# Queueing the uses of gathered rows behind points of the third and fourth groups, a set number for each point

## The chip, the cores and the metric

The kernel runs on one core of a Trainium2 chip. A core has TensorE for matrix products, VectorE and ScalarE for arithmetic by elements and by rows, GpSimd, which here issues the gathers, and SyncE, which issues most of the other transfers; 16 DMA engines carry all transfers. The metric is the device time of one execution in microseconds (us). Before the change it is 3744.16 us, the median of three runs from 3742.86 to 3752.52.

## The reference

One layer of a diffusion backbone over 1024 latent tokens and 256 context tokens, in float32, with 1024 channels. Only the latent stream is put out.

```python
z_lat = modulate(h_lat, sh_a, sc_a) @ w_in          # and z_ctx
att_lat = block_attention(q_l, concat([k_c, k_l]), concat([v_c, v_l]))   # 8 heads, 1280 keys
s5_lat, s5_ctx = s5_mixer(...)                      # state-space branch, two directions
merged = sigmoid(gate_mla) * att + sigmoid(gate_s5) * s5_out
h_lat = layer_norm(ALPHA * h_lat + g_a * (merged @ w_out))
f_lat = peer(modulate(h_lat, sh_f, sc_f), ...)
h_lat = layer_norm(ALPHA * h_lat + g_f * f_lat)
```

The part that matters here is `peer`. For each token 8 heads choose 16 of 16384 experts each, so 128 experts. Expert e has a row u[e] and a row v[e] of 1024 numbers. The output of a token is the sum over its experts of g * gelu(u[e] . x) * v[e].

## The kernel before

The 1024 tokens are eight blocks of 128, handled in four groups: `GROUPS = ((0,), (1, 2), (3, 4, 5), (6, 7))`. For each group `front` traces, in this order: `attention` (eight heads, and for each head and block one pass over 1280 keys: score matmuls, row maximum, exponential, transposes, product with the values), `gates` (four column slices, and in each the blocks of the group), `close` (output projection, two layer norms, and the next group's query projection in `prepare`), and then `route`, a generator that finds each token's 128 experts. The routing of a group is stepped inside the attention of the next: two steps after each head (`TSTEP`). Inside the gates of the third and fourth groups `spread` steps, which writes the gates of the routed experts into dense tables, mostly on ScalarE with small matmuls on TensorE.

The experts are applied in three ways. Blocks 2 to 5 (`DENSE`) multiply with all experts in `dense`, which runs last and takes about the last 40% of the time. Blocks 6 and 7 (`VEC`) are gathered beside it. Blocks 0 and 1 are gathered beside the groups, in `retrieve([0, 1])`, and this is what the change touches. In `score` (L1264 on) each of 128 steps gathers one row u for each of the block's 128 tokens (an indirect DMA on GpSimd's queue, 128 rows of 4 KB, L1269), and VectorE multiplies it with the tokens and sums (L1273): one use. In `weighted` each of 128 steps gathers rows v (L1349), and TensorE adds them, weighted, into two banks with four matmul calls (L1354): one use as well. All rows land in one pool of six buffers (`RB = 6`), so a gather waits until the use of the row six before it is done. The order in which `retrieve` traces the uses is: 128 scores of block 0, then 32 weighted rows of block 0, then two scores of block 1 to one weighted row of block 0, then the remaining weighted rows, those of block 1 last. The weighted rows of a block need all of its scores.

The order in each engine's queue is made when the program is built: a list scheduler goes through the traced instructions with an estimate of their times, and where an engine is free it takes the ready instruction of the best priority. `retrieve([0, 1])` is traced after the fourth group's `front`, which is traced under `tc.high_priority` (`PRIO`), so its uses come behind all work of the groups and fill what that leaves. On the chip each queue then runs in that order. `tc.issue_after(ins)` adds an edge to each instruction of its block that is on the engine of `ins`: it is placed in the queue behind `ins`, with no wait for its end.

Before the change such edges stand on scores alone, by `HOLDS`: block 0's first 36 scores are free and the others are behind `p2`, the end of the third group's query projection (`prepare(2)`, L774); block 1's first 100 are free and the others are behind `p3`, that of the fourth group. The entries that name steps of routing (`r1`, `r2`) begin at 164 and 228 and so hold nothing. The uses of block 6 are behind `t3`. The weighted rows on TensorE have no edge.

```python
HOLDS = {0: [(M0, S0)] + [("r1.%d" % h, S0 + P0 * (h + 1)) for h in range(8)],
         1: [(M1, S1)] + [("r2.%d" % h, S1 + P1 * (h + 1)) for h in range(8)],
         6: [("t3", 0)]}
```

Of the kernel before, what the change touches and what calls it, by code (L numbers as in the profile page):

```python
# [17 lines left out]
MUL, ADD, SUB = ALU.mult, ALU.add, ALU.subtract  # L18
# [57 lines left out]
P1 = 128  # L76
M0 = "p2"
M1 = "p3"
HOLDS = {0: [(M0, S0)] + [("r1.%d" % h, S0 + P0 * (h + 1)) for h in range(8)],
         1: [(M1, S1)] + [("r2.%d" % h, S1 + P1 * (h + 1)) for h in range(8)],  # L80
         6: [("t3", 0)]}
KENG = ((), (), (), ())
GENG = ((), (), (), ())
EVERY = (1, 2, 1)
# [4 lines left out]
def block_kernel(ctx: ExitStack, tc: tile.TileContext, a: dict, out: bass.AP):  # L89
# [91 lines left out]
            marks["last"] = V.scalar_tensor_tensor(x, x, rstd[:, j:j + 1], b, op0=MUL, op1=ADD)  # L181

    marks = {}

    def transpose8(x, put, tag="tp"):

        for h in range(2):
            pt = bank(tag, "tp", (128, 4, 128))
            for j in range(4):
                k = 4 * h + j  # L190
                PE.transpose(pt[:, j, :], x[:, k * 128:(k + 1) * 128], eye)
            put(h, pt)


# [40 lines left out]
    def product(o, x, w, n):  # L235

        for k in range(n):
            PE.matmul(o, x[0][:, k, :], w[0][:, k, :], start=(k == 0), stop=False)
            PE.matmul(o, x[1][:, k, :], w[0][:, k, :], start=False, stop=False)
            PE.matmul(o, x[0][:, k, :], w[1][:, k, :], start=False, stop=(k == n - 1))  # L240


    xt = []
# [544 lines left out]
    def attention(grp, att):  # L788
        nt = len(grp)
        ntok = 128 * nt  # L790
        Q, cqT, rq = R["q"]
        A = pool("A")
        late = []

        def finish(P, sm3, vt, i, h):

            rs = cols.tile([128, 1], F32, tag="smx", name="smx")
            V.tensor_reduce(rs, sm3, axis=AX.X, op=ADD)
            V.reciprocal(rs, rs)
            PT = A.tile([128, NT, 128], F32, tag="PT", name="PT")  # L800
            for b0, b1 in ((0, 4), (4, 8), (8, 10)):
                pt = bank("tp", "pt", (128, 4, 128))
                for j in range(b0, b1):
                    PE.transpose(pt[:, j - b0, :], P[:, j * 128:(j + 1) * 128], eye)
                S.copy(PT[:, b0:b1, :], pt[:, 0:b1 - b0, :])
            po = bank("mm", "po")
            for j in range(NT):
                PE.matmul(po[:, 0:128], PT[:, j, :], vt[:, j, :], start=(j == 0), stop=(j == NT - 1))  # L808
            S.activation(att[i][:, h * 128:(h + 1) * 128], po[:, 0:128], func=AF.Copy, scale=rs)

        for pr in range(4):
            qn = []
            qr = A.tile([128, ntok], F32, tag="qr", name="qr")
            rl = A.tile([128, ntok], F32R, tag="rl", name="rl")
            q2 = rl.bitcast(F32)
            wq = wload(a["w_uq"][pr], [128, 3, 512])
            for j in (2, 3, 0, 1):
                ps = bank("mm", "pq")
                for k in range(3):
                    PE.matmul(ps[:, 0:ntok], wq[:, k, j * 128:(j + 1) * 128], cqT[:, k, :], start=(k == 0), stop=(k == 2))  # L820
                if j < 2:
                    qh = A.tile([128, ntok], F32R, tag="qnh", bufs=2, name="qnh")
                    ql = A.tile([128, ntok], F32R, tag="qnl", bufs=2, name="qnl")
                    split(qh, ql, ps[:, 0:ntok])
                    qn.append((qh, ql))
                else:
                    V.tensor_tensor(qr if j == 2 else q2, ps[:, 0:ntok], rq[:, j - 2, :], op=MUL)
            V.tensor_tensor(qr, qr, q2, op=ADD)
            rh = A.tile([128, ntok], F32R, tag="rh", name="rh")
            split(rh, rl, qr)  # L830
            for hh in range(2):
                h = 2 * pr + hh
                lo = 64 * hh
                st = A.tile([128, ntok], F32R, tag="qst", bufs=2, name="qst")
                S.copy(st[0:64], rh[lo:lo + 64].bitcast(F32))
                V.tensor_copy(st[64:128], rl[lo:lo + 64].bitcast(F32))
                kt = wload(k_d[h], [128, KEYS])
                kc = []
                for c in range(3):
                    c0, w = 512 * c, (512 if c < 2 else 256)  # L840
                    kh = A.tile([128, w], F32R, tag="kh%d" % c, name="kh")
                    kl = A.tile([128, w], F32R, tag="kl%d" % c, name="kl")
                    split(kh, kl, kt[:, c0:c0 + w], GP if c in KENG[GROUPS.index(grp)] else V)
                    kc.append((kh, kl))
                vt = A.tile([128, NT, 128], F32, tag="vt", bufs=2, name="vh")
                SY.dma_start(vt, v_d[h])
                qh, ql = qn[hh]
                for i in range(nt):
                    ts = slice(i * 128, (i + 1) * 128)
                    mx = cols.tile([128, 3], F32, tag="mx", name="mx")  # L850
                    pS = []
                    for c in range(3):
                        c0, w = 512 * c, (512 if c < 2 else 256)
                        cs = slice(c0, c0 + w)
                        ps = bank("S", "pS")[:, 0:w]
                        kh, kl = kc[c]
                        PE.matmul(ps, qh[:, ts], kh, start=True, stop=False)
                        PE.matmul(ps, ql[:, ts], kh, start=False, stop=False)
                        PE.matmul(ps, qh[:, ts], kl, start=False, stop=False)
                        PE.matmul(ps, st[:, ts], kpe_h[:, cs], start=False, stop=False)  # L860
                        PE.matmul(ps, st[:, ts], kpe_l[:, cs], start=False, stop=True)
                        V.reduce_max(mx[:, c:c + 1], ps, axis=AX.X)
                        pS.append(ps)
                    mb = cols.tile([128, 1], F32, tag="mb", name="mb")
                    V.reduce_max(mb, mx, axis=AX.X)
                    V.tensor_scalar(mb, mb, -SCALE, None, op0=MUL)
                    P = A.tile([128, KEYS], F32, tag="P", bufs=2, name="P")
                    sm3 = cols.tile([128, 3], F32, tag="sm3", name="sm3")
                    for c in range(3):
                        c0, w = 512 * c, (512 if c < 2 else 256)  # L870
                        S.activation(P[:, c0:c0 + w], pS[c], func=AF.Exp, scale=SCALE, bias=mb,
                                     accum_out=sm3[:, c:c + 1])
                    late.append((P, sm3, vt, i, h))
                    if len(late) > 1:
                        finish(*late.pop(0))
                yield
        finish(*late.pop(0))
        A.release()

    def gates(gi, A, grp, att):  # L880
# [22 lines left out]
        for j in range(4):  # L903
# [12 lines left out]
            for i in range(nt):  # L916
# [5 lines left out]
                V.scalar_tensor_tensor(tg[:, 512:768], tg[:, 512:768], 1.0, pb[:, 0:256], op0=ADD, op1=MUL)  # L922
                V.scalar_tensor_tensor(tg[:, 512:768], tg[:, 256:512], 1.0, tg[:, 512:768], op0=ADD, op1=MUL)
                V.scalar_tensor_tensor(att[i][:, cs], tg[:, 0:256], 1.0, att[i][:, cs], op0=ADD, op1=MUL)
                V.scalar_tensor_tensor(att[i][:, cs], tg[:, 512:768], 0.5, att[i][:, cs], op0=MUL, op1=ADD)
                yield

    def close(gi, B, H, grp, mT):
# [18 lines left out]
        for i, l in enumerate(grp):  # L947
# [20 lines left out]
                evac(hT[:, 4 * h:4 * h + 4, :], pt)  # L968

            transpose8(x, put)  # L970
            if l in DENSE:
                S.dma_start(h2T_d[l], hT.rearrange("p k t -> p (k t)"))
            if "late" in R:
# [288 lines left out]
    def score(l, ei, dots):  # L1262

        pp, rows = R["pp"], R["rows"]  # L1264
        h2 = pp.tile([128, D], F32, tag="h2", bufs=H2B, name="h2")
        SY.dma_start(h2, h2_d[l])
        for s in range(128):
            ub = rows.tile([128, D], F32, tag="row", name="ub")
            GP.indirect_dma_start(out=ub, out_offset=None, in_=a["peer_u"],  # L1269
                                  in_offset=bass.IndirectOffsetOnAxis(ap=ei[:, s:s + 1], axis=0))  # L1270
            held = [m for m, n in HOLDS[l] if s >= n] if l in HOLDS else []
            with tc.issue_after(marks[held[-1]].ins) if held else nullcontext():
                V.scalar_tensor_tensor(ub, ub, 1.0, h2, op0=MUL, op1=MUL, accum_out=dots[:, s:s + 1])  # L1273
            yield

# [22 lines left out]
    def weighted(l, ei, eiT, g, dots):  # L1298
# [25 lines left out]
        else:  # L1324
# [14 lines left out]
            for b in range(8):  # L1339
# [5 lines left out]
                for jj in range(4):  # L1345
                    for q in range(4):
# [2 lines left out]
                        GP.indirect_dma_start(out=vb, out_offset=None, in_=a["peer_v"],  # L1349
                                              in_offset=bass.IndirectOffsetOnAxis(ap=eiT[:, t:t + 1], axis=0))  # L1350

                        for d in range(4):
                            o = 32 * ((q + d) % 4)
                            PE.matmul(acc[d // 2][o:o + 32, 256 * (d % 2):256 * (d % 2) + 256], dg[:, q, jj, :],  # L1354
                                      vb[:, d * 256:(d + 1) * 256], start=False, stop=False,
                                      tile_position=(0, o))
                        yield
            nothing(False)

# [230 lines left out]
```

## Time and profile before

| | us |
|---|---|
| median of three runs | 3744.16 (3742.86 to 3752.52) |
| the profiled execution, its own time | 3758.78 |
| its span, first to last instruction | 3757.0 |
| VectorE busy | 2889.2 |
| ScalarE busy | 1496.5 |
| GpSimd busy | 1477.3 |

The page has the busy time of each engine over the whole span, the span in 40 slices, and the costliest groups of instructions. A busy time is the union of the instructions' times. Idle time in front of an instruction is put down to what ended it: for instance `PE acc L1354 <- DMA vb` is time in which TensorE stood idle until a gathered row had landed. PE is TensorE, DVE is VectorE, ACT is ScalarE, POOL is GpSimd; PEld are TensorE's weight loads. The view by stretch cuts the span at times that are given and shows each engine's busy time in each (in brackets the instructions), TensorE's granted clock as a share of full speed, the mean busy share of the DMA engines, and GB/s.

### The profile page before, as it was taken

What the parts mean: (1) busy time and instruction counts of PE and PEld (TensorE: products, weight loads), DVE (VectorE), ACT (ScalarE), POOL (GpSimd) and SP (SyncE); (2) the same over time, 40 slices, a digit from 0 to 9 for tenths busy, and PEclk for the clock granted to TensorE, in tenths of its full rate; (3) what the DMA queues carried; (4) which work ended last, traced back from release to release, by engine and by line L of the source; (5) the groups of instructions that cost most, each with busy time, mean ns of one, the idle gap of its engine ahead of it and who ended that gap; (6) DMA issues with size and microseconds to landing.
All of it is one profiled execution on the core that took longest, in us unless ns stands there. A gap on an engine that the chain in (4) does not pass through costs nothing.

```text
span 3757.0 us, 54909 instructions
## 1 busy us (share of the span) xinstructions
PE 3376.1 (90%) x20022; PEld 2741.5 (73%) x20022; DVE 2889.2 (77%) x6864; ACT 1496.5 (40%) x2967; POOL 1477.3 (39%) x1254
## 2 busy tenths in 40 slices
PE   5968888979779889879989879999999999999997
PEld 3745577869667669667659668788888888888885
DVE  7357755685898877789846667888888888889985
ACT  2223353443123457133359794333333333333332
POOL 5035400041355553454441300465555555546530
PEclk7978999989889989989999989999999999999998
DMA  8652276476698888887887854699999999989972
GB/s 279 230 87 72 89 263 225 157 296 244 230 341 312 311 334 334 339 325 286 292 328 272 323 206 163 236 359 339 343 336 337 332 335 339 340 319 355 338 272 73
DMA packets 348718, 1032.49 MB, mean 275 GB/s; under 512 B 46592, under 2 KB 142080, under 8 KB 322592
## 3 DMA queue, kind: packets, MB, share of 16 engines
q0 software_dynamic: 147456, 536.94, 39.0%
q1 hardware_dynamic: 164032, 462.20, 34.7%
q10 hardware_dynamic: 36960, 29.86, 2.5%
q8 instruction: 157, 2.57, 0.3%
q14 instruction: 113, 0.93, 0.1%
HBM read 961.27 MB, written 67.62 MB: 274 GB/s over the span
## 4 chain that ended last, share of the span: by engine, by line
PE 56%; DVE 9%; issue 7%; DMA 5%; ACT 4%; POOL 2%; SPq 0%; DVEq 0%; ACTq 0%; POOLq 0%
PE turn L1233 6%; PE turn L1234 6%; PE turn L1235 6%; PE fd L1194 5%; PE fd L1195 5%; PE fd L1196 5%; DMA ub<-in_peer_u,ei 2%; PE pqr L1065 2%; DVE ub L1273 2%; PE acc L1354 2%; PE pe L1151 2%; DMA vb<-in_peer_v,eiT 2%; PE po L808 2%; PE po L953 1%; POOL ub L1269 1%
## 5 line engine op out<-in xcount | busy, mean ns | idle before, releaser
L1269 POOL DMA_INDIRECT ub<-in_peer_u,ei x512 | 639.6, 1249 | 1221.7 <-DVE ub L1273 446.8
L1273 DVE SCALAR_TENSOR_TENSOR ub<-ub,h 128x1024 f32<-128x1024 f32 x512 | 617.0, 1219 | 52.4 <-DMA ub<-in_peer_u,ei 46.5
L1316 POOL DMA_INDIRECT vb<-in_peer_v,ei x256 | 363.4, 1420 | 266.3 <-DVE f L1319 203.6
L1349 POOL DMA_INDIRECT vb<-in_peer_v,eiT x256 | 288.4, 1126 | 402.8 <-PE acc L1354 313.5
L1233 PE MATMUL turn<-hh,u 128*128 128x512 f32 x1024 | 400.9, 392 | 1.2 <-ACT act L1237 1.2
L1234 PE MATMUL turn<-hh,u 128*128 128x512 f32 x1024 | 400.5, 391 | 0.1
L1235 PE MATMUL turn<-hl,u 128*128 128x512 f32 x1024 | 399.9, 390 | 0.0
L1195 PE MATMUL fd<-v,kpe_l 128*128 128x512 f32 x891 | 353.5, 397 | 3.6 <-DVE kpe_l L233 3.6
L1196 PE MATMUL fd<-v,kpe_h 128*128 128x512 f32 x891 | 351.1, 394 | 0.0
L1194 PE MATMUL fd<-v,kpe_h 128*128 128x512 f32 x891 | 341.5, 397 | 0.0
L1319 DVE SCALAR_TENSOR_TENSOR f<-vb,zz,f 128x1024 f32<-128x1024 f32 x254 | 325.7, 1282 | 3.1 <-DMA vb<-in_peer_v,ei 0.4
L1237 ACT ACTIVATE act<-turn 128x512 f32<-128x512 f32 x128 | 76.6, 598 | 588.0 <-PE turn L1235 587.9
L232 ACT CAST v<-w 128x1024 fp32r<-128x1024 f32 x128 | 134.8, 1053 | 282.9 <-PE fd L1195 279.4
L1233 PEld LDWEIGHTS turn<-hh,u 128*128 128x128 f32 x1024 | 192.2, 188 | 44.1 <-ACT act L1237 1.4
L1235 PEld LDWEIGHTS turn<-hl,u 128*128 128x128 f32 x1024 | 192.3, 188 | 41.9
L1234 PEld LDWEIGHTS turn<-hh,u 128*128 128x128 f32 x1024 | 192.2, 188 | 41.1 <-DVE u L233 0.4
L1354 PE MATMUL acc<-vb,diag 128*32 128x256 f32 x2048 | 164.5, 402 | 49.0 <-DMA vb<-in_peer_v,eiT 45.8
L1148 DVE TENSOR_SCALAR second<-iota,pl 128x128 f32<-128x128 f32 x512 | 141.4, 350 | 81.4 <-PE pe L1151 74.7
L1195 PEld LDWEIGHTS fd<-v,kpe_l 128*128 128x128 f32 x891 | 167.5, 188 | 43.4 <-DVE kpe_l L233 4.6
L1196 PEld LDWEIGHTS fd<-v,kpe_h 128*128 128x128 f32 x891 | 167.6, 188 | 41.5
L1194 PEld LDWEIGHTS fd<-v,kpe_h 128*128 128x128 f32 x891 | 167.3, 188 | 40.7
L233 DVE TENSOR_TENSOR v<-w,v 128x1024 fp32r<-128x1024 f32 x128 | 156.6, 1223 | 43.4 <-ACT v L232 42.7
(422 smaller groups left out, 8254.2 us busy)
## 6 DMA issues: line engine op xcount, KB each, us to landing
w<-in_peer_uT SPq DMA_DIRECT2D x64, 1024.0 KB
w<-in_peer_v SPq DMA_DIRECT2D x64, 1024.0 KB
w<-in_peer_wq SPq DMA_DIRECT2D x32, 1024.0 KB
gT_d<-stage SPq DMA_DIRECT2D x16, 2048.0 KB
gt<-gT_d SPq DMA_DIRECT2D x32, 1024.0 KB
vh<-v_d SPq DMA_DIRECT2D x32, 640.0 KB
w<-k_d SPq DMA_DIRECT2D x32, 640.0 KB
w<-in_w_mod_b SPq DMA_DIRECT2D x16, 1024.0 KB
```

What stands on the lines that cost most here:

```text
L1194: PE.matmul(o, ah[:, ts], vh[:, cs], start=first, stop=False)
L1195: PE.matmul(o, al[:, ts], vh[:, cs], start=False, stop=False)
L1196: return PE.matmul(o, ah[:, ts], vl[:, cs], start=False, stop=final)
L1233: PE.matmul(turn, uh[:, k, :], hh[:, k, :], start=(k == 0), stop=False)
L1234: PE.matmul(turn, ul[:, k, :], hh[:, k, :], start=False, stop=False)
L1235: PE.matmul(turn, uh[:, k, :], hl[:, k, :], start=False, stop=(k == 7))
L1269: GP.indirect_dma_start(out=ub, out_offset=None, in_=a["peer_u"], in_offset=bass.IndirectOffsetOnAxis(ap=ei[:, s:s + 1], axis=0))
L1273: V.scalar_tensor_tensor(ub, ub, 1.0, h2, op0=MUL, op1=MUL, accum_out=dots[:, s:s + 1])
L1316: GP.indirect_dma_start(out=vb, out_offset=None, in_=a["peer_v"], in_offset=bass.IndirectOffsetOnAxis(ap=ei[:, s:s + 1], axis=0))
L1319: V.scalar_tensor_tensor(f, vb, z[:, s:s + 1], f, op0=MUL, op1=ADD)
L1349: GP.indirect_dma_start(out=vb, out_offset=None, in_=a["peer_v"], in_offset=bass.IndirectOffsetOnAxis(ap=eiT[:, t:t + 1], axis=0))
L1354: PE.matmul(acc[d // 2][o:o + 32, 256 * (d % 2):256 * (d % 2) + 256], dg[:, q, jj, :], vb[:, d * 256:(d + 1) * 256], start=False, stop=Fal ...
```

## The change

The holds on blocks 0 and 1 go. In their place `pace` notes, at each point of the third group (index 2) and of the fourth (index 3), a pair of instructions, one on VectorE and one on TensorE, as many times as `BESIDE` says for that stage: 7, 6 and 14 for the attention, gates and close of the third group, 8, 6 and 14 for those of the fourth. A point of the attention is one head of one block (the scaling of the row maximum on VectorE, and the first transpose of the exponentials of the pass before on TensorE); a point of the gates is one block of one column slice (the last merge on VectorE and the last product on TensorE); a point of the close is one block (the last step of its second layer norm, and the last transpose). `paced` counts the uses of blocks 0 and 1 in the order in which they are traced, scores and weighted rows together. The first 36 (`FREE`) have no edge; use number n after them is queued behind the n-th noted pair, on its own engine. The gathers themselves get no edge.

```diff
-HOLDS = {0: [(M0, S0)] + [("r1.%d" % h, S0 + P0 * (h + 1)) for h in range(8)],
-         1: [(M1, S1)] + [("r2.%d" % h, S1 + P1 * (h + 1)) for h in range(8)],
-         6: [("t3", 0)]}
+HOLDS = {6: [("t3", 0)]}
+FREE = 36
+BESIDE = {2: (7, 6, 14), 3: (8, 6, 14)}
...
+    paces = []
+
+    def pace(gi, stage, v):
+
+        if gi in BESIDE:
+            paces.extend([(v, marks["PE"])] * BESIDE[gi][stage])
+
+    def paced(engine):
+
+        n = marks["n"] = marks.get("n", -1 - FREE) + 1
+        return tc.issue_after(paces[min(n, len(paces) - 1)][engine].ins) if n >= 0 else nullcontext()
...
-                    PE.transpose(pt[:, j - b0, :], P[:, j * 128:(j + 1) * 128], eye)
+                    mm = PE.transpose(pt[:, j - b0, :], P[:, j * 128:(j + 1) * 128], eye)
+                    if not j:
+                        marks["PE"] = mm
...
-                    V.tensor_scalar(mb, mb, -SCALE, None, op0=MUL)
+                    ready = V.tensor_scalar(mb, mb, -SCALE, None, op0=MUL)
...
+                    pace(GROUPS.index(grp), 0, ready)
...
-                V.scalar_tensor_tensor(att[i][:, cs], tg[:, 512:768], 0.5, att[i][:, cs], op0=MUL, op1=ADD)
+                pace(gi, 1, V.scalar_tensor_tensor(att[i][:, cs], tg[:, 512:768], 0.5, att[i][:, cs], op0=MUL, op1=ADD))
...
             transpose8(x, put)
+            pace(gi, 2, marks["last"])
...
             held = [m for m, n in HOLDS[l] if s >= n] if l in HOLDS else []
-            with tc.issue_after(marks[held[-1]].ins) if held else nullcontext():
+            with (tc.issue_after(marks[held[-1]].ins) if held else nullcontext() if l in VEC else paced(0)):
                 V.scalar_tensor_tensor(ub, ub, 1.0, h2, op0=MUL, op1=MUL, accum_out=dots[:, s:s + 1])
...
-                        for d in range(4):
-                            o = 32 * ((q + d) % 4)
-                            PE.matmul(acc[d // 2][o:o + 32, 256 * (d % 2):256 * (d % 2) + 256], dg[:, q, jj, :],
-                                      vb[:, d * 256:(d + 1) * 256], start=False, stop=False,
-                                      tile_position=(0, o))
+                        with paced(1):
+                            for d in range(4):
+                                o = 32 * ((q + d) % 4)
+                                PE.matmul(acc[d // 2][o:o + 32, 256 * (d % 2):256 * (d % 2) + 256], dg[:, q, jj, :],
+                                          vb[:, d * 256:(d + 1) * 256], start=False, stop=False,
+                                          tile_position=(0, o))
```

The lines left out set `marks["PE"]` in the transposes and products of the groups.

## Rows read from the trace of the kernel before

**Rows 1.** Head of the page: span, busy time of each engine.
```profile
span 3757.0 us, 54909 instructions
...
PE 3376.1 (90%) x20022; PEld 2741.5 (73%) x20022; DVE 2889.2 (77%) x6864; ACT 1496.5 (40%) x2967; POOL 1477.3 (39%) x1254
```

**Rows 2.** Stretch, length; busy PE, PEld, DVE, ACT, POOL; clock, DMA share, GB/s.
```profile
985.00:1013.50 28.50, 15.25 (x42) 9.16 (x42) 24.93 (x47) 4.61 (x11) 17.58 (x14) 0.74 0.89 335
1013.50:1081.00 67.50, 64.68 (x492) 60.58 (x493) 63.13 (x186) 26.10 (x69) 39.85 (x35) 0.96 0.92 332
1081.00:1122.00 41.00, 21.35 (x92) 13.87 (x90) 40.66 (x151) 7.02 (x18) 19.60 (x20) 0.82 0.95 354
1155.00:1242.00 87.00, 80.11 (x663) 60.25 (x663) 75.78 (x382) 26.88 (x72) 35.12 (x35) 0.96 0.76 275
1282.30:1300.80 18.50, 16.86 (x106) 10.83 (x104) 14.46 (x35) 6.92 (x18) 12.24 (x12) 1.00 0.94 325
1340.00:1403.00 63.00, 46.82 (x362) 41.15 (x361) 43.37 (x85) 39.18 (x78) 29.50 (x25) 0.84 0.91 346
1403.00:1517.00 114.00, 113.48 (x986) 105.84 (x985) 87.46 (x197) 86.42 (x174) 46.59 (x40) 1.00 0.85 314
1645.00:1914.00 269.00, 252.25 (x1937) 192.11 (x1937) 227.46 (x1050) 103.50 (x252) 121.56 (x111) 0.98 0.82 295
1979.00:2260.00 281.00, 245.31 (x1932) 214.22 (x1931) 184.79 (x643) 251.58 (x558) 45.87 (x43) 0.93 0.68 259
2500.00:3600.00 1100.00, 1100.00 (x4762) 889.86 (x4761) 967.50 (x1182) 364.45 (x499) 626.70 (x453) 1.00 0.93 337
```

**Rows 3.** The same view of the scores of gathered rows (L1273) alone, VectorE.
```profile
985.00:1340.00 355.00, 157.43 (x259) 0.93 0.88 321
985.00:1013.50 28.50, 18.01 (x30) 0.74 0.89 335
1013.50:1081.00 67.50, 42.50 (x70) 0.96 0.92 332
1081.00:1122.00 41.00, 23.15 (x38) 0.82 0.95 354
1155.00:1242.00 87.00, 5.05 (x10) 0.96 0.76 275
1340.00:1403.00 63.00, 17.95 (x31) 0.84 0.91 346
1403.00:1517.00 114.00, 33.08 (x54) 1.00 0.85 314
1645.00:1914.00 269.00, 18.22 (x30) 0.98 0.82 295
```

**Rows 4.** The same view of the weighted rows (L1354) alone: TensorE, weight loads.
```profile
985.00:1340.00 355.00, 30.48 (x408) 10.53 (x408) 0.93 0.88 321
1403.00:1517.00 114.00, 8.95 (x112) 2.20 (x112) 1.00 0.85 314
1645.00:1914.00 269.00, 58.05 (x768) 19.14 (x768) 0.98 0.82 295
```

**Rows 5.** Waits, 985 to 1914 us: us in total, times, longest.
```profile
PE acc L1354 <- DMA vb<-in_peer_v,eiT: 36.2, 14, 7.0
PE pS L857 <- ACT P L871: 25.6, 9, 8.7
...
DVE ub L1273 <- DMA ub<-in_peer_u,ei: 30.1, 21, 4.5
```

**Rows 6.** Attention points (L866), third and fourth group: duration ns, first and last start.
```profile
L866 DVE TENSOR_SCALAR mb<-mb x24: 130/148/155, 1013.5 to 1339.6; 128x1 f32<-128x1 f32 x24
...
L866 DVE TENSOR_SCALAR mb<-mb x16: 125/146/154, 1645.1 to 1914.1; 128x1 f32<-128x1 f32 x16
```

**Rows 7.** Chain of waits around 998 us: start, us, what.
```profile
998.25 10.03 DMA ub<-in_peer_u,ei
```

More of the change, by code (lines that the diff above doesn't have):

```diff
@@ L190, in transpose8 @@
                 k = 4 * h + j
-                PE.transpose(pt[:, j, :], x[:, k * 128:(k + 1) * 128], eye)
+                marks["PE"] = PE.transpose(pt[:, j, :], x[:, k * 128:(k + 1) * 128], eye)
             put(h, pt)
@@ L239, in product @@
             PE.matmul(o, x[1][:, k, :], w[0][:, k, :], start=False, stop=False)
-            PE.matmul(o, x[0][:, k, :], w[1][:, k, :], start=False, stop=(k == n - 1))
+            marks["PE"] = PE.matmul(o, x[0][:, k, :], w[1][:, k, :], start=False, stop=(k == n - 1))
     xt = []
@@ L860, in attention @@
                         PE.matmul(ps, st[:, ts], kpe_h[:, cs], start=False, stop=False)
-                        PE.matmul(ps, st[:, ts], kpe_l[:, cs], start=False, stop=True)
+                        marks["PE"] = PE.matmul(ps, st[:, ts], kpe_l[:, cs], start=False, stop=True)
                         V.reduce_max(mx[:, c:c + 1], ps, axis=AX.X)
```

## The prediction

> **What bounds the kernel now.** I read the head of the page first, then the busy time of each engine by stretch, then the waits, then the chain. The reader is to see in [rows 1] a span of 3757.0 us with TensorE busy for 90% of it. The table of stretches [rows 2] shows that this share is not even: from 2500 to 3600 us TensorE never rests (1100.00 of 1100.00 us), and nothing in the change touches that part, so it only moves earlier or later as a whole. The change works between 985 us, where the third group's attention begins, and the end of the fourth group. In its attention TensorE idles in spots: at 985 to 1013.5 us it is busy for 15.25 of 28.5 us, at 1081 to 1122 us for 21.35 of 41, and in the second of these VectorE is busy for 40.66. The scores of gathered rows are the reason to look at: the same stretches restricted to them [rows 3] hold 18.01 and 23.15 us of VectorE. Each score stands there as two entries (the product with its sum, and the reading of the sum), so x259 at 985 to 1340 us are 129 scores of 1.22 us. The weighted rows on TensorE [rows 4] are eight entries each: x408 are 51, of 0.60 us.
>
> The waits [rows 5] name two losses: 36.2 us in which TensorE stood before a weighted row that had not landed, and 25.6 us in which its next score matmuls waited for the softmax of the block before (longest 8.7 us); VectorE stood for 30.1 us before rows that had not landed. A queue's order is fixed when the program is built, so what stands behind such a use waits too.
>
> **What the change does to the counts.** 36 uses stay free, as now. The other 476 are queued behind points: 7 for each of the 24 points of the third group's attention, 6 for each of 12 gate points, 14 for each of 3 closing points; then 8, 6 and 14 for 16, 8 and 2 points of the fourth group: 282 and 204 places. The order of uses stays: 92 scores, 32 weighted rows, then two scores to one weighted row until the scores end, then weighted rows alone. No instruction, transfer or byte is added or removed. The points of the kernel before are in [rows 6]: the third group's attention has them from 1013.5 to 1339.6 us, the fourth's from 1645.1 to 1914.1 us. The edge is one of queue order alone, so no engine gets a new semaphore wait; gathers stay unheld, but six buffers tie them to the uses.
>
> Now the sum, stretch by stretch; the numbers of 1 to 9 are from [rows 2 to 4]. A score that goes takes 1.22 us off VectorE; what the stretch gains is bounded by what else it needs.
>
> 1. *985 to 1013.5 us.* 15 scores stand here, ahead of the first point; none may after. That leaves 6.9 us on VectorE and 15.25 on TensorE, the latter at a granted clock of 0.74. The nearest row is 1282.3 to 1300.8 us, which also opens a pair of heads and carries no routing: 18.5 us. I take that: **-10 us** (bounds 0, and -13 for TensorE alone).
> 2. *1013.5 to 1081 us.* 35 scores now, five points with 7 each after: **0**. TensorE is busy for 64.68 of 67.5.
> 3. *1081 to 1122 us.* 19 scores become 7: 14.6 us less, VectorE's sum falls to 26.0. At the load that VectorE has in the first stretch (24.93 of 28.5) this takes 30 us: **-11 us** (bounds 0 and -14.6).
> 4. *1155 to 1242 us.* Here the change adds. Now 5 scores stand beside 70.7 us of other VectorE work (routing); five points allow 35, or 42.7 us, 113.4 in all for 87 us. If all run in place this costs 27 us; if they are left until VectorE has room, nothing, since they are last in priority. The weighted rows that fill TensorE here now (80.11 of 87) go later, which frees TensorE. I take **+5** (bounds 0 and +27), nearer to waiting, since the scheduler takes a use only when nothing of the front is ready.
> 5. *1340 to 1403 us.* 15 scores and some weighted rows become 7 uses in all. The transfers, 0.91 of their engines' time, then carry the gates' weights with fewer gathers beside them. TensorE idles 16.2 us here; I take a little over a third: **-6** (bounds 0 and -16).
> 6. *1403 to 1517 us.* 27 scores and 14 weighted rows become up to 66 uses, 25 more, of them 8 weighted rows on a TensorE that is busy for 113.48 of 114: **+5**. The bounds are 0 and +21: 25 gathers of 0.52 MB at the 346 GB/s of the row before are 38 us of transfer, on top of 0.85 of 114.
> 7. *1517 to 1645 us.* 48 uses are allowed, 14 behind each closing point: **0**, for want of a row that speaks for either sign.
> 8. *1645 to 1914 us.* 15 scores and 96 weighted rows become at most 23 and 97. Eight more scores are 9.8 us on a VectorE busy for 227.46 of 269: **+4** (bounds 0 and +10).
> 9. *After 1914 us.* ScalarE is busy for 251.58 of the 281 us to 2260, TensorE for 245.31: the weighted rows that move here lie beside ScalarE's work: **0**. Without that cover, 20 rows cost 12 us.
> 10. *Waits for rows.* When a burst starts, up to six rows have had the time since the last point to land. Of the 36.2 us on TensorE [rows 5] I take a quarter off, since another part of them lies in the stretches counted above: **-9** (bounds 0 and -36).
>
> Before the 24th point 161 uses are allowed where 180 are done now, so the points do bind; the 19 go to the gates. What is late next in the third group is routing on VectorE (70.7 of 87 us without scores).
>
> Sum: -10 - 11 + 5 - 6 + 5 + 4 - 9 = **-22 us**. On the profiled span that is 3735. The profiled run took 3758.78 us, the median of the three runs is 3744.16; I set the same 22 us against the median: **3722 us**.
>
> One price on which the trace and the Trainium skill differ is that of a row asked for late. The row first: the chain [rows 7] has a gather that takes 10.03 us from the end of its issue to its landing, in the crowded stretch at 998 us. A burst of seven scores has six buffers, so the seventh row is asked for only when the first score is done, and seven scores end 7.3 us later: by the row it would be some 4 us late. The Trainium skill, in "DMA: Bandwidth & Descriptors", section "Anatomy of one DMA — SWDGE (gpsimd) path", gives a transfer of this kind about 2.0 us plus its bytes over 436 GB/s, by which a gather of 0.52 MB (128 rows of 4 KB) takes an estimated 3.2 us and the seventh row would be in time. By that page the burst costs nothing and the sum stays at -22.
>
> **Rivals.**
> - *A set number does not ask what a point carries.* Scores fall into the routing stretch (4) at their full price, the gates (6) run out of transfer time, and (8) pays in full, while only (1) and (3) gain: -21 + 27 + 21 + 10 = +37, so 3781 us. For it: VectorE has 70.7 us of other work in 87. Against it: uses come last in priority and may slip to later points. It decides from the point where more than half of the 35 scores of stretch 4 are issued before its routing ends.
> - *The seventh row of a burst is late.* At 4 us for each of some 22 bursts of the third group's attention, 88 us on the sum above: +66, 3810 us. Against it: all uses of today go over the same six buffers, and VectorE stood for them 30.1 us in 21 waits, not 88.
> - *It changes nothing that counts.* The allowed numbers come within 20 of the present ones in each stage, and what one stretch gains the next pays, or the uses lag behind their points so that the points hold nothing back: within 11 us of 3744. For it: VectorE is busy for 128.7 of the first 137 us [rows 2], so work that leaves one place finds little room in another.
> - *All of these losses go.* Terms 1, 3, 5 at their bounds and the whole of 36.2: -13 - 14.6 - 16 - 36 = -80, 3664 us. Against it: transfers run at 0.76 to 0.95 of their engines' time in these stretches, so rows cannot all be early.
>
> **How the numbers follow.** The forecast (3700 to 3732 us) gets 0.42, the larger gain 0.13, no change 0.20, the uneven load 0.20, the late seventh row 0.05. A measurement of this kernel tells about 0.3%, 11 us, from no change. Faster is 0.42 + 0.13 = 0.55, same 0.20, slower 0.25. The range leaves out most of the -80 case below and, above, the late row and the worse part of the uneven load: 3680 to 3785 us.
>
> **What would show it.** Up to 985 us the trace should be the same. The first attention point of the third group should come about 10 us earlier after its projection, with no score ahead of it; the stretch between the sixth and the seventh point (now 1081 to 1122 us) should be near 30 us; TensorE's wait for weighted rows should fall below 30 us; and the dense part should start some 20 us earlier and be as long as now. It is wrong if the third group's attention is longer than its present 326 us between its first and last point, if VectorE's wait for rows grows beyond 40 us, or if the dense part starts later.

## The result, and the profile after

The changed kernel takes 3789.05 us (median of four runs, 3779.05 to 3795.14) where the kernel before takes 3745.45 (four runs, 3742.86 to 3752.52): the ratio is 1.0106, with a 95% interval from 1.0089 to 1.0123. It is slower by some 44 us, and the forecast was 22 us faster. Executions of one kernel lie 10 to 30 us apart, and each profile below is one of them, so a difference of under some 5 us in one stage is not read.

The head of the page, as in [rows 1]: TensorE's busy time is 17 us more, VectorE's the same.

```profile
span 3793.4 us, 54903 instructions
...
PE 3393.4 (89%) x20022; PEld 2750.6 (73%) x20022; DVE 2887.8 (76%) x6864; ACT 1493.9 (39%) x2965; POOL 1486.0 (39%) x1254
```

The attention points as in [rows 6], both groups in one row; there are 24 and then 16, and the third group's last is at 1327.9 us, the fourth's first at 1623.3.

```profile
L879 DVE TENSOR_SCALAR mb<-mb x40: 115/146/154, 997.5 to 1932.0; 128x1 f32<-128x1 f32 x40
```

The same view by stretch as [rows 2], cut at the same events: start of the third group's attention to its first point, first to sixth point, sixth to seventh, tenth to fourteenth (from the ninth in [rows 2]), lead-in of the gates (from the last attention point to the first gate point), the gates, the fourth group's attention, and from the first point of its gates to the end of the spread.

```profile
980.00:997.50 17.50, 14.09 (x42) 8.53 (x42) 8.15 (x17) 4.61 (x11) 0.00 (x0) 0.78 0.42 160
997.50:1064.50 67.00, 56.13 (x402) 52.32 (x403) 59.84 (x157) 24.42 (x65) 40.79 (x34) 0.92 0.87 311
1064.50:1099.80 35.30, 28.56 (x181) 22.73 (x181) 34.00 (x182) 8.87 (x23) 9.77 (x9) 1.00 0.74 273
1139.70:1222.00 82.30, 60.61 (x367) 51.53 (x365) 81.20 (x330) 23.10 (x60) 33.10 (x27) 0.85 0.64 232
1327.90:1387.90 60.00, 46.61 (x370) 40.63 (x371) 43.27 (x89) 41.15 (x83) 29.89 (x24) 0.89 0.93 361
1387.90:1502.30 114.40, 113.29 (x980) 105.99 (x979) 89.04 (x195) 85.47 (x170) 46.21 (x39) 1.00 0.86 318
1623.30:1932.00 308.70, 268.77 (x1906) 202.44 (x1907) 252.94 (x1094) 104.98 (x253) 140.33 (x129) 0.92 0.82 293
1993.80:2296.70 302.90, 255.72 (x2090) 214.25 (x2089) 187.63 (x662) 251.88 (x560) 62.39 (x60) 0.94 0.71 271
```

The scores alone (L1288, as [rows 3], two entries for a score): third group's attention with its start, the sixth to the seventh point, the tenth to the fourteenth, the gates, the fourth group's attention.

```profile
980.00:1327.90 347.90, 128.24 (x214) 0.92 0.78 278
1064.50:1099.80 35.30, 8.50 (x16) 1.00 0.74 273
1139.70:1222.00 82.30, 33.43 (x56) 0.85 0.64 232
...
1387.90:1502.30 114.40, 33.92 (x56) 1.00 0.86 318
1623.30:1932.00 308.70, 45.05 (x74) 0.92 0.82 293
```

The weighted rows alone (L1370, as [rows 4], eight entries for a row): the same attention, one step of it late in that stretch, the gates, the fourth group's attention, and from its last point to the end of the spread.

```profile
980.00:1327.90 347.90, 24.70 (x320) 8.52 (x320) 0.92 0.78 278
1256.30:1288.60 32.30, 11.72 (x156) 4.09 (x156) 1.00 0.94 338
1387.90:1502.30 114.40, 8.30 (x104) 2.05 (x104) 1.00 0.86 318
1623.30:1932.00 308.70, 59.92 (x736) 18.65 (x736) 0.92 0.82 293
1932.00:2296.70 364.70, 58.07 (x696) 19.12 (x696) 0.94 0.74 282
```

The waits, 980 to 1932 us, as [rows 5].

```profile
PE acc L1370 <- DMA vb<-in_peer_v,eiT: 43.8, 22, 8.2
...
PE pS L870 <- ACT P L884: 28.2, 9, 5.9
...
DVE ub L1288 <- DMA ub<-in_peer_u,ei: 25.6, 18, 5.7
```

What the reader is to see: the third group's attention with its start holds 107 scores and 40 rows where it held 129 and 51. The gates take 28 and 13 where they took 27 and 14, so the missing uses are not made up there. 22 of them arrive in the fourth group's attention: 37 scores where 15 were, and 308.7 us where 269 were. From its last point to the end of the spread, called the tail below, 87 rows (x696) are left; that stretch takes 364.7 us, and before it took 345.7 with 72 rows. Here is the kernel before, all engines and then the rows alone:

```profile
1914.10:2259.80 345.70, 299.13 (x2413) 255.29 (x2411) 214.60 (x717) 299.49 (x661) 72.72 (x66) 0.93 0.72 274
...
1914.10:2259.80 345.70, 48.36 (x576) 16.57 (x576) 0.93 0.72 274
```

The 36.4 us between the two spans are 39.6 in the fourth group's attention, 19.0 behind it, 4.3 between the third group's first and last point, less 11.0 ahead of the first point, 10.1 from the third group's last point to the fourth's first, 4.9 ahead of 985 us (where nothing was changed) and some 0.5 in the dense part.

### The profile page after: what moved, and what is told of

Its sections match the earlier page's. It is cut to its first block, busy times and chain, and to the rows that moved or that the text cites. A ratio compares the mean times of both kernels' runs of the same rounds, so it can differ in the third digit from the quotient of the medians.

```text
span 3793.4 us, 54903 instructions
## 1 busy us (share of the span) xinstructions
PE 3393.4 (89%) x20022; PEld 2750.6 (73%) x20022; DVE 2887.8 (76%) x6864; ACT 1493.9 (39%) x2965; POOL 1486.0 (39%) x1254
## 4 chain that ended last, share of the span: by engine, by line
PE 57%; DVE 8%; issue 7%; DMA 6%; ACT 4%; POOL 2%; SPq 0%; DVEq 0%; ACTq 0%; POOLq 0%
PE turn L1248 6%; PE turn L1249 6%; PE turn L1250 6%; PE fd L1210 5%; PE fd L1209 5%; PE fd L1211 5%; DMA vb<-in_peer_v,eiT 3%; PE pqr L1080 2%; PE pe L1166 2%; DVE ub L1288 2%; PE acc L1370 2%; DMA ub<-in_peer_u,ei 2%; PE po L967 2%; PE po L821 1%; PE pg L249 1%
## 5 line engine op out<-in xcount | busy, mean ns | idle before, releaser
L1284 POOL DMA_INDIRECT ub<-in_peer_u,ei x512 | 661.4, 1292 | 1203.6 <-DVE ub L1288 486.0
L1288 DVE SCALAR_TENSOR_TENSOR ub<-ub,h 128x1024 f32<-128x1024 f32 x512 | 614.2, 1217 | 48.2 <-DMA ub<-in_peer_u,ei 46.0
L1364 POOL DMA_INDIRECT vb<-in_peer_v,eiT x256 | 277.3, 1083 | 435.7 <-PE acc L1370 357.2
L1370 PE MATMUL acc<-vb,diag 128*32 128x256 f32 x2048 | 169.6, 405 | 58.9 <-DMA vb<-in_peer_v,eiT 58.8
```

## The experiments

Theory: the points starve block 0 (they hold its scores back), and the kernel pays for it twice. With no score ahead of the first point and seven a point, block 0's last score comes at the 14th point, behind the third group's routing; its weighted rows miss the room that TensorE has there; the mixture of scores and rows starts late; scores that are left over fall into the fourth group's routing, and rows that are left over into the tail. The rivals are told with each run. Three series ran, each on one chip with the kernel before beside it: 3758.72, 3745.24 and 3756.71 us there.

**Nine a point** (cap9, first series).

```diff
-BESIDE = {2: (7, 6, 14), 3: (8, 6, 14)}
+BESIDE = {2: (9, 6, 14), 3: (8, 6, 14)}
```

> Nine instead of seven uses for each attention point of the third group, all else as changed. Theory (starved, then paid twice): seven a point hold back some 33 uses in the third group's attention; gates and close cannot take them, so 22 scores land in the routing of the fourth group's attention (+40 us) and some 19 weighted rows behind its close (+24 us). With nine, the queues hold about as many uses by the end of that attention as before the change, and 15 scores from the fourth group's first point on: its attention takes 265 to 275 us again, the first step to 17 us stays, the total is 3722 to 3740 us. Rival (pacing itself costs, wherever): the fourth group's attention stays above 295 us and the total above 3770.

It took 3771.05 us, 1.0028 [1.0012, 1.0044] of before. The fourth group's attention is back at 270.8 us with 15 scores, so the starving is undone; the total is not the one expected. The start kept its gain (18.4 us to the first point), but the attention took 343.7 us between its points where 326.1 had done: of the 15 scores that left the start 11 are issued between its points, and the other 4 in the gates and their lead-in, which take 9.9 us more. That these scores are what the added time goes to is not shown.

**No points in the fourth group** (no4).

```diff
-BESIDE = {2: (7, 6, 14), 3: (8, 6, 14)}
+BESIDE = {2: (7, 6, 14)}
```

> The points of the fourth group taken away, those of the third kept; the queues are the same up to the end of the fourth group's attention. Theory: the fourth group's points hold next to nothing back, so the time is that of the changed kernel within 12 us (3775 to 3795), attention of the fourth group 300 us or more. Rival (the fourth group's eight a point starve TensorE and push rows behind its close): below 3760, and the stretch from the last close to the last dense-table matmul back at 115 us.

It took 3810.47 us, 1.0132 [1.0095, 1.0169], with 309.8 us in the fourth group's attention: that group's own points are not the cause. (The total is above the 3795 us of the theory; by its ratio to the kernel before, whose median is 13 us higher on this chip, it agrees with the change's 1.0106 within the intervals.)

**The kernel before, made late by hand** (hold78): block 1's scores from the 79th on behind the fourth group's projection, no points.

```diff
-S1 = 100
+S1 = 78
```

> The kernel before, with no points at all; only the hold on block 1's scores starts at 78 instead of 100, so that 36 scores instead of 15 stand from the fourth group's first point on, 20 of them in its long routing step. Theory: that alone costs what the change cost there: attention of the fourth group 300 to 315 us, some 40 weighted rows left after the close, total 3785 to 3810 us, more than the changed kernel since the third group's start does not gain its 11 us. Rival (points or edges on TensorE cost): within 11 us of before (3735 to 3757).

It took 3787.1 us, 1.0073 [1.0056, 1.0091]. Without any point it has what the change has: 36 scores and 303.6 us in the fourth group's attention, then 87 rows and 362.1 us to the end of the spread. The scores there, and the rows behind:

```profile
1621.10:1924.80 303.70, 43.98 (x72) 0.93 0.82 292
```

```profile
1924.80:2286.90 362.10, 59.06 (x696) 19.54 (x696) 0.95 0.75 284
```

(The third group's closing stage, with no score, is 22 us shorter, 74.5 for 96.3.) The long step between the fourth group's fourth and fifth point, which carries the most routing, shows the price. All engines, then the scores alone: before, after, this version, and nine a point.

```profile
1686.60:1737.70 51.10, 47.42 (x347) 38.35 (x347) 49.59 (x280) 14.80 (x32) 22.88 (x20) 1.00 0.86 322
...
1686.60:1737.70 51.10, 4.86 (x8) 1.00 0.86 322
```

```profile
1660.70:1736.10 75.40, 58.66 (x351) 47.61 (x349) 69.17 (x303) 17.35 (x35) 40.15 (x35) 0.86 0.89 321
...
1660.70:1736.10 75.40, 25.55 (x42) 0.86 0.89 321
```

```profile
1660.00:1735.20 75.20, 55.27 (x339) 44.55 (x337) 65.86 (x290) 17.05 (x34) 36.23 (x33) 0.87 0.88 323
...
1660.00:1735.20 75.20, 24.47 (x40) 0.87 0.88 323
```

```profile
1703.40:1756.50 53.10, 48.01 (x332) 38.60 (x331) 49.59 (x278) 14.01 (x31) 20.77 (x20) 0.94 0.79 288
...
1703.40:1756.50 53.10, 4.85 (x8) 0.94 0.79 288
```

VectorE is busy for 49.59 of the 51.1 us before, so a score has no gap to fall into. 17 more scores lengthen the step by 24.3 us, of which 19.6 are VectorE's busy time. The granted clock falls from 1.00 to 0.86, a mean between the 2.4 GHz level and the 1.2 GHz one, in a step where TensorE now rests for 16.7 us and rested for 3.7. In the three versions with 20 or 21 scores in this step it takes 75.2 to 76.6 us, in the other nine, with 0 to 6, it takes 45.5 to 59.8.

The scores do not explain all of the 39.6 us. From the seventh point to the last, neither kernel has a score, and that stretch is 14.3 us longer, at a lower granted clock and with VectorE as busy as it was. All engines, before and after:

```profile
1758.70:1914.10 155.40, 145.06 (x1138) 105.23 (x1138) 124.48 (x577) 57.62 (x148) 68.20 (x65) 0.97 0.80 284
```

```profile
1762.30:1932.00 169.70, 150.40 (x1160) 103.59 (x1159) 126.67 (x577) 57.10 (x146) 73.33 (x73) 0.93 0.78 279
```

What lengthens it no run tells.

**The last 42 rows behind the last close** (late_w), to see whether rows are dear for standing in the tail.

```diff
+LATE = 86
...
-                PE.transpose(pt[:, j, :], x[:, k * 128:(k + 1) * 128], eye)
+                marks["PE"] = PE.transpose(pt[:, j, :], x[:, k * 128:(k + 1) * 128], eye)
...
+            marks["w%d" % gi] = marks["PE"]
...
+                        with tc.issue_after(marks["w3"].ins) if l == 1 and 16 * b + 4 * jj + q >= LATE else nullcontext():
```

> The kernel before, with the last 42 weighted rows of block 1 queued behind the last transpose of the fourth group's close, as many as the changed kernel leaves there. Theory: the stretch from the end of the last close to the last dense-table matmul grows from 114 to 130 to 140 us and most of that shows at the end: total 3755 to 3770 us. Rival (that stretch is set by ScalarE, the rows lie beside it): within 11 us of before, stretch 110 to 120 us.

3757.82 us, 0.9998 [0.9981, 1.0014]: the theory of this run fell. 40 rows now stand between the close and the end of the spread, and the tail has not grown (340.2 us). Where the rows stand within the tail costs nothing; that they are more may.

**Rows held out of the fourth group's attention** (left30, second series): the kernel before, with block 1's rows from the 31st on behind that group's last pass.

```diff
+LATE = 30
...
-                    PE.transpose(pt[:, j - b0, :], P[:, j * 128:(j + 1) * 128], eye)
+                    mm = PE.transpose(pt[:, j - b0, :], P[:, j * 128:(j + 1) * 128], eye)
+                    if not j:
+                        marks["PE"] = mm
...
+                        with tc.issue_after(marks["PE"].ins) if l == 1 and 16 * b + 4 * jj + q >= LATE else nullcontext():
```

> The kernel before, with the weighted rows of block 1 from its 31st on queued behind the last attention pass of the fourth group: 165 rows in place of 196 stand ahead of that pass's end, and no score moves. Theory 3 (the time from the fourth group's last point to the end of the spread goes by the number of rows that are left, as 87 for 72 went with 19 us more in the changed kernel): about 103 rows left, that time 375 to 390 us in place of 346, the fourth group's attention 240 to 255 in place of 269, in all 5 to 20 us slower. Theory 4 (the added 19 us are not the rows' but come from the routing and the spread being later or at a lower clock): that time stays within 5 us of 346, and the kernel is 15 to 25 us faster.

3771.9 us, 1.0075 [1.0056, 1.0093]. The rows alone (L1358) in the fourth group's attention and behind it:

```profile
1639.50:1899.80 260.30, 41.41 (x560) 14.08 (x560) 0.96 0.72 259
1899.80:2266.80 367.00, 62.28 (x784) 21.53 (x784) 0.96 0.78 296
```

70 rows where 96 were, and 98 where 72 were. The attention is 8.8 us shorter, the stretch behind it 21.3 longer: a row costs 0.3 us in the attention and 0.8 us behind it. Theory 3 holds in its direction (367.0, a little under its 375). The counts of the other runs agree in order: 81 rows go with 352.6 us (every3, below), 87 with 362.1, 364.7 and 368.0 (hold78, the change, no4), and 68 to 73 with 340 to 349 (all others). They give no single price: the change's 15 rows more go with 19.0 us, 1.3 us a row, and left30's 26 with 21.3.

**More free uses** (free51 and free69, second series; free84, third). The points stay as in the change.

```diff
-FREE = 36
+FREE = 51
```

> The change with 51 free uses for 36, so that 15 scores may again stand ahead of the third group's first attention point; the points keep their numbers. In the queues block 0's last score now stands before the routing step of the third group's attention that starts near 1188 us (in the changed kernel behind it), and 243 scores for 219 stand ahead of the fourth group's attention. Theory 1 (the change loses because block 0's last scores come behind that routing step, so the weighted rows miss TensorE's room beside it and the mixture of scores and rows starts late): first point at 28 us after the projection, fourth group's attention near 270 us (not 309), the stretch from its last point to the end of the spread near 346 (not 365), and in all within 0.3% of the kernel before. Theory 2 (a set number for each point costs by itself, by rows that land late): third group's attention over 335 us between its points and 10 to 20 us slower in all.

3765.16 us, 1.0057 [1.0037, 1.0077]. Two of the four numbers of theory 1 came: 267.6 us for the fourth group's attention and 344.0 behind it. The 316.6 us between the third group's points speak against theory 2, which had over 335. The first point comes after 17 us, not 28, since the 15 scores more stand ahead of the projection; and the total missed: the gates took 143.6 us with 36 scores and 16 rows, where 114.8 had done. Their waits:

```profile
POOL ub L1284 <- PE acc L1370: 22.9, 4, 12.9
POOL vb L1364 <- PE acc L1370: 21.1, 6, 11.2
...
DVE tg L936 <- ACT tg L935: 13.1, 4, 10.3
ACT tg L927 <- DVE att L939: 11.9, 1, 11.9
DVE ub L1288 <- DMA ub<-in_peer_u,ei: 11.2, 2, 6.5
```

GpSimd stands before its next gathers until TensorE has used rows, VectorE stands before a score whose gather came late, and the gates' own steps stand behind one another. Which of these links starts the rest is not settled.

```diff
-FREE = 36
+FREE = 69
```

> The change with 69 free uses for 36: 33 scores ahead of the third group's first point, and two more ahead of its last than in the kernel before. Theory 1: the fourth group's attention has 11 scores in place of 15, so 265 to 270 us; what is saved later is paid ahead of the first point, where 33 scores take 40 us of VectorE alone (28.5 us now): in all 0 to 10 us slower than before, and 25 to 40 faster than the change. Theory 2: the third group's attention again over 335 us.

3745.03 us, 0.9999 [0.9986, 1.0012]: the loss is gone. 33 uses more run ahead of the projection, not ahead of the first point as expected. From the second group's last point to the projection, all engines and then the scores, before and here:

```profile
840.90:984.90 144.00, 130.63 (x944) 124.38 (x942) 83.40 (x191) 37.21 (x57) 13.24 (x10) 0.95 0.58 202
...
840.90:984.90 144.00, 11.85 (x20) 0.95 0.58 202
```

```profile
834.90:985.00 150.10, 130.46 (x944) 123.85 (x942) 118.58 (x258) 37.33 (x57) 64.15 (x43) 0.96 0.83 312
...
834.90:985.00 150.10, 51.46 (x86) 0.96 0.83 312
```

33 scores more (x86 for x20) take 6 us. Block 0's last score comes between the ninth and the tenth point, as it does in the kernel before. The rows beside the third group's routing (eleventh to fourteenth point), before, after and here:

```profile
1175.80:1242.00 66.20, 18.34 (x256) 7.54 (x256) 1.00 0.75 266
```

```profile
1151.10:1222.00 70.90, 0.00 (x0) 0.00 (x0) 0.85 0.59 208
```

```profile
1148.40:1223.30 74.90, 19.36 (x256) 7.22 (x256) 0.98 0.73 251
```

All 32 rows of block 0 that open its sum lie here in the kernel before and in this version, and none in the change. The fourth group's attention has 11 scores and 259.5 us; none of them is in its long step, which takes 45.5 us. Its profiled execution (3731.70 us) is the shortest of its twelve, and that of the kernel before (3758.78) is longer than all four of its runs, so single stages flatter this version; the medians decide.

```diff
-FREE = 36
+FREE = 84
```

> The change with 84 free uses for 36: block 0's last score comes at the seventh point, and 15 more scores than with 69 free stand ahead of the projection. Theory A (what decides is that block 0 is done before the routing step, and early scores lie beside TensorE's projection for a third of their price, as 18 scores made that stretch 6 us longer): 0 to 10 us faster than the kernel before, third group's attention 300 to 312 us. Theory C (VectorE fills up ahead of the projection: 114 of its last 145 us were busy with 69 free, and 15 scores of 1.22 us are 18 more): that stretch grows by 12 to 18 us, and the kernel is 0 to 12 us slower than before.

3762.88 us, 1.0012 [0.9998, 1.0027]: theory C. The stretch ahead of the projection is now 166.7 us, 16.6 longer than with 69, and pays for the rest.

**The early scores without the points** (s0_54, third series).

```diff
-S0 = 36
+S0 = 54
```

> The kernel before with 54 free scores of block 0 for 36, and no points: 69 scores stand ahead of the third group's first attention point, as in the version with points and 69 free uses, and the long step between its sixth and seventh point keeps 21 scores. It tells the points from the earlier scores. Theory A (the points are worth nothing by themselves; that version came back to the time of before because its scores stand ahead of the routing step): within 0.3% of the kernel before, 3735 to 3755 us on a chip where that has 3745; third group's attention 312 to 322 us between its points, fourth group's 265 to 272. Theory B (the even spacing earns some 10 us, which the early scores cost): 8 to 15 us slower than the kernel before, with the long step at 40 us or more.

3757.6 us, 1.0002 [0.9986, 1.0017]: theory A in the total. (The third group's attention, 330.2 us, and the fourth's, 274.5, are longer than A gave, and the third group's long step, from its sixth to its seventh point, is 45.9, as B gave it.) With points and without them, early scores end at the time of the kernel before: the even spacing earned nothing by itself.

**Three scores to a row** (every3, second series).

```diff
-EVERY = (1, 2, 1)
+EVERY = (1, 3, 1)
```

> The kernel before with three scores of block 1 to one weighted row of block 0 in place of two, so that scores end sooner: 8 scores in place of 15 in the fourth group's attention, 248 in place of 241 ahead of it, and 12 scores more among the gates of the third group, where VectorE has room (87 of 114 us busy). Theory 1 (a score is cheap beside the gates and dear in routing): fourth group's attention 258 to 265 us, 5 to 12 us faster in all. Rival (a use costs the same wherever it stands): within 4 us of the kernel before.

3764.96 us, 1.0052 [1.0035, 1.0069], slower, which neither side expected. The fourth group's attention has 8 scores and 103 rows, and takes 270.7 us; what the scores left, rows fill, and 81 rows are left behind it. No version beat the kernel before.

## Why the prediction was wrong

It took the third group's end for the place where left-over uses vanish: "the 19 go to the gates". 33 were left over, and the gates, the lead-in and the close took what they take in the kernel before. From there two terms fell.

- Term 8, "15 scores and 96 weighted rows become at most 23 and 97", +4: measured 37 and 92, and +39.6 us. This is the largest error. hold78 comes to much the same, 36 scores and 303.6 us, with no point at all, and free69 takes both away while it keeps every point. The price of a score, 1.22 us of VectorE, was right; in the long routing step it is paid in full, and the granted clock is lower there besides. That step is 24.3 of the 39.6 us; 14.3 stand behind the seventh point, in steps without a score, and their cause stays open.
- Term 9, after 1914 us, 0: measured +19.0 with 15 rows more. ScalarE's work was not the cover it was taken for; left30 gives 0.8 us a row, where the prediction had 12 us for 20 rows without that cover. At that price 15 rows are 12 of the 19 us, and the rest is not accounted for.
- Term 1, -10: measured -11.0, as the opening row of another pair of heads gave it.
- Term 2, 0: measured -0.5. Term 3, -11: -5.6 (35.3 us, where 30 were forecast). The seven scores stand there as forecast, but VectorE is busy for 34.00 us, not 26.0: without its scores it did 17.5 us of work there before and does 25.5 now, as more of the routing comes into the room.
- Term 4, +5: the ninth to the fourteenth point take 97.0 us for 87, so +10, and scores were issued there and did not wait for room: 28 between the tenth and the fourteenth point. (Its upper bound of +27 is 26.4 by its own figures.) What the term left out is the other side: the 32 rows went to later points, where one step alone holds 19 of them (x156) and takes 32.3 us.
- Terms 5 to 7, -6, +5 and 0: measured -3.0, -0.4 and, with the lead-in to the fourth group's attention, -6.7.
- Term 10, -9: TensorE's wait for rows is 43.8 us for 36.2. Bursts did not help it.

The rival of uneven load had the right sign and about the right time (3781 us) from the wrong places: it charged the third group's routing and gates, and the bill came one group later. Its point of decision, that more than half of 35 scores are issued in the routing stretch, did come about. The rival of the late seventh row fell: VectorE waited for rows for 25.6 us, less than before. Its price rested on one gather of 10.03 us. In the trace of the change the gathers for scores from 980 to 1932 us land as follows, from the start of the issue, which itself takes 0.94 us in the median:

```profile
DMA to landing us min/median/max: 4.1/6.7/15.3
```

The prediction's burst leaves a seventh row some 6 us (10.03 less the 4 it would be late), so the gather in the middle would be late by less than 1 us, not by 4; the 10.03 us were far above the middle. By the Trainium skill, "DMA: Bandwidth & Descriptors", section "Anatomy of one DMA — SWDGE (gpsimd) path", the seventh row would be in time, with an estimated 3.2 us for a gather; the waits agree, but here only the quickest gathers come near that figure.

The failing could be read ahead of the run. 92 scores at seven a point need 13.1 points, so the last of them stands behind the routing that the kernel before gives to rows; the prediction named both facts and did not put them together. It counted uses without their kinds and order.

What stays open is what starts the 29 us in the gates of free51, why 9 a point costs the third group's attention 17.6 us for 11 scores more between its points, and what the 14.3 us of term 8 and the rest of term 9 go to.

## What to carry to other kernels

Where an even quota replaces a greedy fill (take whatever is ready), ask at which point the quota finishes each kind of work and what that completion unlocks: here block 0's last score came at the fourteenth point instead of just ahead of the tenth, and 32 weighted rows stayed out of the one stretch that had room for them. Follow the left-over to where it really lands, and price it there: a stage that is full takes no more because it is allowed to, and here the next routing step, with VectorE busy throughout, paid the full duration. A cover by another engine's busy share is to be tested by count (more rows in that stretch), not assumed.

## What the runs showed of the hardware

The gathered scores cost very different amounts by place: 33 more beside the projection made it 6 us longer, while a routing step with 17 more was 24.3 us longer, and the granted TensorE clock fell there from 1.00 to 0.86 although TensorE had nearly the same work (x351 for x347).
